# Nine regions instead of seven with a last product in quarters; the sums' room taken from s2, which is read back from DRAM; A in runs of 512 columns

## The chip, the cores and the metric

The kernel runs on one core of a Trainium2 chip. The metric is the device time of one execution in microseconds (us), the median of several runs.

## The reference

```python
m, k, n = 4096, 4096, 4096
x = np.matmul(a, b)                      # a, b: float32
return np.where(x > 0, x, alpha * x)     # alpha = 0.01
```

## The kernel before, in words

**Stages.** The inputs are rounded to fp16 on their way in. A is handled in four groups `g` of 1024 rows, B in four blocks `j` of 1024 columns. The 16 pairs (g, j) are done one after the other. The pair (0, 0) is done first in a stage of its own with plain products (line L295); the other 15 are called regions and come in this order: (0,1), (0,2), (0,3); (1,2), (1,0), (1,1), (1,3); (2,2), (2,0), (2,3), (2,1); (3,2), (3,0), (3,1), (3,3). In this text they are regions 0 to 14. The last region of each group is "turning": while it computes, the next group's A is loaded. Region 14 is the last one.

**A region.** It is one 2 x 2 step of a fast matrix product with seven products in place of eight. The four quarters of the group's A are a11, a12, a21, a22, each [512 rows x 2048 of k], in two tiles (k halves u); the four quarters of the block of B are b11, b12, b21, b22, each in two tiles of 1 MiB. Sums s1 to s4 of A's quarters are made on VectorE (DVE) once per group, sums of B's quarters in place in every region (`b_sum`, L574). The products (`PRODUCTS`), each 64 matmuls of 128 x 512 (L691), are numbered 0 to 6: a11 b11, a12 b21, s2 with a b11 sum, s3 with a b12 sum, s1 with another b11 sum, a22 with a b21 sum, s4 b22. Four PSUM banks `y` and four banks `z` take them in turn; ScalarE (ACT) copies a bank out (`keep`, L704), DVE adds (`add`, L746), applies the leaky step (L323), and SP stores.

**Quarters.** Where `in_quarters` holds, product 6 is split once more into seven parts of 16 matmuls of 128 x 256 (`quarters_product`, L722): 112 narrow matmuls in place of 64 wide ones. For that it needs sums of quarters of b22 (`tq`, four DVE operations in `sums_b`, L655 to L658) and of s4 (`sq`, made in the group's first region by `sums_s4` and kept in DRAM as `kept_s`; read back on SP in later regions). In the kernel before this holds in regions 3, 4, 7, 8, 11, 12 and 13. The room for `tq` and one `sq` is taken from b12's tiles (pool tag b12), so in these regions b12 of the next region can't be loaded before product 6 is done.

**Loads.** B and A come over POOL's queue, which converts fp32 to fp16: B in DMAs of 512 KiB (`fetch_unit`, two for a tile), A through staging tiles (pool a16, three of them, 4 KiB in a partition each, four DMAs each; L128) that DVE then transposes into place (L137). In group's first regions the block j = 2 of B is read back, already in fp16, from the DRAM copy `kept` on SP's queue. `fetch_b(i + 1, ...)` loads a quarter of the next region's B when the product that last reads it is done: b12 after product 3, b11 after 4, b21 after 5, b22 after 6; in quarter regions b12's two tiles come after product 6 too, mixed with b22's. In a turning region a11 of the next group is fetched and transposed after product 0's sums, a12 after product 1, a21 after 3, a22 after 5 (`fetch_a`). Each is four pieces; the fourth needs the staging tile of the first, so it is fetched when the first has been transposed. All engines work in the order of the program, and in turning regions DVE's order is: sums b12 and b11 (first k half, then second), transposes of a11, add and leaky of product 1, sum b21, transposes of a12, second sum b11, transposes of a21.

The second sum b11 (called b11'' here) must be there for product 4, the first one for product 2.

**Measuring.** The kernel also gathers the spread of the squares of every quarter of A and B (`Measure`: four ACT squares, about six DVE operations, held in a16 tiles) for a check at the end. `MEASURED` lists which quarter is measured where. Quarters of b that the region's in-place sums would have overwritten are measured a region ahead (entries `fifth`, `sixth`), or, twice, loaded a second time only to be measured (`MeasureApart`).

Of the kernel before, what the change touches and what calls it, by code (L numbers as in the profile page):

```python
# [8 lines left out]
P = 128  # L9
# [15 lines left out]
KC = 8  # L25
KW = KC * P
KU = 4
RUNS = [2, 1]
NT = 512
MT = 4  # L30
# [14 lines left out]
def kernel(  # L45
# [61 lines left out]
    def new_a(g, h, u):  # L107
        if (g, h, u) not in at:
            tag = f"a{h + 1}{u // 2 + 1}"
            at[g, h, u] = a_pool.tile([P, KC // 2, RM, 2], DT, name=tag, tag=tag)  # L110
        return at[g, h, u]
# [32 lines left out]

    def pieces_a(g, h, u, urgent=False):

        if u >= 2:
            return [whole_half(g, h, mt) for mt in range(MT) if u == 2]
        tiles = 2 * RUNS[u]
        kw = KW // RUNS[u]  # L150

        def piece(mt, tiles, r):
            def to(t0, t1):
                rows = slice((mt + t0) * P, (mt + t1) * P)
                return [new_a(g, h, u)[:, r * kw // P // 2:(r + 1) * kw // P // 2, rows, :]]
            row = ((g * 2 + h) * MT + mt) * P
            return load_a(row, u * KW + r * kw, kw, tiles, to)

        pieces = [piece(mt, tiles, r) for mt in range(0, MT, tiles) for r in range(RUNS[u])]
        if urgent:  # L160
            pieces[:1] = [piece(mt, 2, 0) for mt in range(0, MT, 2)]
        return pieces

    def whole_half(g, h, mt):
        def to(t0, t1):
            rows = slice((mt + t0) * P, (mt + t1) * P)
            return [new_a(g, h, u)[:, :, rows, :] for u in (2, 3)]
        return load_a(((g * 2 + h) * MT + mt) * P, 2 * KW, 2 * KW, 1, to)

    def b_rows(j, u, c, wide, nt=None):  # L170

        if u >= 2:
            per = 2 * KC
            k0 = 2 * KW
            c += u % 2 * KC
        else:
            per = KC // RUNS[u]
            k0 = u * KW + c // per * per * P
        n0 = j * 2 * NT + (nt or 0) * NT
        cols = slice(n0, n0 + (2 * NT if nt is None else NT))  # L180
        src = b[k0:k0 + per * P, cols].rearrange("(p c) n -> p c n", p=P)
        return src[:, c % per:c % per + wide, :]

    def load_b(j, u, c, wide, nt):
        nc.gpsimd.dma_start(new_b(j, u, nt)[:, c:c + wide, :], b_rows(j, u, c, wide, nt))
# [22 lines left out]
    class Measure:  # L208
# [12 lines left out]
        def square(self, n):  # L221
            to = self.place(n)
            nc.scalar.activation(to, self.parts[n], SQUARE)  # L223
            self.held.append(to)
# [5 lines left out]
        def end(self):  # L230
# [3 lines left out]
            nc.vector.tensor_add(total, total, more[1])  # L234
            nc.vector.tensor_add(total, total, self.held[3])  # L235
            fold(self.which, total, self.place(2), self.pairs)

    class MeasureApart(Measure):

        def load(self):
            self.loaded = [self.fetch(n) for n in range(3)]

        def fetch(self, n):
            to = self.place(n)
            half, nt, jb = self.parts
            nc.gpsimd.dma_start(
                to.bitcast(DT).rearrange("p (c n) -> p c n", n=NT),
                b_rows(jb, 2 * half + n // 2, n % 2 * 4, 4, nt))  # L250
            return to

        def square(self, n):
            to = self.loaded[n] if n < 3 else self.fetch(n)
            nc.scalar.activation(to, to.bitcast(DT), SQUARE)  # L255
            self.held.append(to)

    def fold(which, total, turned, pairs, weight=1.0):

# [237 lines left out]
            first_measure.end()  # L497


    kept = dram_pool.tile([KU, 2, P, KC * NT], DT, name="kept")  # L500
    regions = [(0, j) for j in range(1, J)]
    regions += [(g, j) for g in range(1, G) for j in ([2, 0, 3, 1] if g == 2 else [2, 0, 1, 3])]

# [8 lines left out]
    def fetch_unit(i, u, nt):  # L512
        g, j = regions[i]
        half = u // 2
        t = b_pool.tile([P, KC, NT], DT, name="b", tag=f"b{half + 1}{nt + 1}")
        have_b[i, u, nt] = t
        if g and j == CACHED:
            nc.sync.dma_start(t.rearrange("p c n -> p (c n)"), kept[u, nt])
        else:
            for c in range(0, KC, 4):  # L520
                nc.gpsimd.dma_start(t[:, c:c + 4, :], b_rows(j, u, c, 4, nt))  # L521
            if j == CACHED:
                nc.sync.dma_start(kept[u, nt], t.rearrange("p c n -> p (c n)"))

    have_b = {(0, u, nt): bt[1, u, nt] for u in range(2) for nt in range(2)}

    s = {}
    first_a = at[0, 0, 0]

    def flat(t):  # L530
# [13 lines left out]
        nc.vector.tensor_tensor(f(to), f(x0), f(x1), op)  # L544

    def new_s(g, name):
        t = x_pool.tile([P, 2, KC // 2, RM, 2], DT, name=name, tag="x")
        for k in range(2):
            s[g, name, k] = t[:, k]
        return t  # L550
# [22 lines left out]
        f = lambda t: t.rearrange("p c n -> p (c n)")  # L573
        nc.vector.tensor_tensor(f(to), f(x0), f(x1), op)  # L574

    def measure(i, which, x, y, jb=None, room=None):

        if jb is not None:
            return MeasureApart(which, (x, y, jb), False)
        if which:  # L580
            tiles = [have_b[i, 2 * x + k, y] for k in range(2)]
        else:
            tiles = [at[regions[i][0], x, 2 * y + k] for k in range(2)]
        parts = halves(tiles[0]) + halves(tiles[1])
        if tiles[0] is first_a:
            return MeasureFirst(which, parts, None)
        return Measure(which, parts, not which, room)

    def judge():
# [25 lines left out]
    A11, A12, A22 = (0, 0, 0), (0, 0, 1), (0, 1, 1)  # L615
    B11, B12, B21, B22 = ((1, half, nt) for half in range(2) for nt in range(2))
    MEASURED = {
        (0, 1): (None, [A11], B12, B11), (0, 2): (B21, [B22, A22], None, A12),
        (1, 2): (None, [A11], None, None), (1, 0): (B21, [B22, A12], None, None),
        (1, 1): (B21, [B22, A22], B12, B11),  # L620
        (2, 2): (None, [A11], None, None), (2, 0): (A12, [B11 + (0,)], None, None),
        (2, 3): (B21, [B22, A22], B12, B11),
        (3, 2): (None, [A11], None, None), (3, 0): (A12, [A22], None, None),
        (3, 1): (None, [B12 + (0,)], None, None),
    }

    PRODUCTS = [("a11", 0, 0), ("a12", 1, 0), ("s2", 0, 0), ("s3", 0, 1), ("s1", 0, 0), ("a22", 1, 0), ("s4", 1, 1)]


    HALF = NT // 2  # L630
    kept_s = dram_pool.tile([4, P, KC * HALF], DT, name="kept_s")
    side = 0

    def quarter_a(t):
# [1 line left out]

    def rooms(i):

        two = [b_pool.tile([P, 2, KC * HALF], DT, name="q", tag="b12") for _ in range(2)]
        three = [a16_pool.tile([P, KC * HALF], DT, name="sq4", tag="a16") for _ in range(3)]  # L640
        tq = {2: two[0][:, 0], 1: two[0][:, 1], 4: two[1][:, 0]}
        sq = {1: three[0], 2: three[1], 3: three[2], 4: two[1][:, 1]}
        return tq, sq
# [32 lines left out]
    for i, (g, j) in enumerate(regions):  # L676
# [98 lines left out]
        middle = middle and measure(i, *middle)  # L775
        late_ones = [measure(i, *x) for x in late_ones]
        first_of_group = i == 0 or regions[i - 1][0] != g
        next_turning = i + 2 < len(regions) and regions[i + 2][0] != g
        in_quarters = g > 0 and not turning and not next_turning and not final

        product(0, y, True)
        if middle:
            middle.begin()
        u1 = keep(y, side)
# [2 lines left out]
            b_sum(B(0, 0, k), B(0, 1, k), B(0, 0, k), ADD)  # L787
        if middle:
            middle.end()
        apart = late_ones and isinstance(late_ones[0], MeasureApart)  # L790
        if apart:
            late_ones[0].load()
        fetch_a(0, 0)

        product(1, z, True)
# [13 lines left out]
            b_sum(B(0, 0, k), B(1, 1, k), B(0, 0, k), SUB)  # L809
        if first_of_group:  # L810
            sum_a(g, "s4")
        if late_ones and not apart:
            late_ones[0].end()

        z = [new_bank(zbank + mt) for mt in range(MT)]
        product(3, z, True)
        v = keep(z, side)
        if not in_quarters:
            fetch_b(i + 1, [(0, 1)])
        fetch_a(1, 0)  # L820
        if apart:
            late_ones[0].end()
        for m in late_ones[1:]:
            m.begin()
            m.end()
        if in_quarters:
            tq, sq = rooms(i)
            if first_of_group:
                sums_s4(g, sq)
                sums_b(i, tq)  # L830

        product(4, y, False)
        a21 = None
        if turning:
            new_s(g + 1, "s1")
            t = new_s(g + 1, "s2").rearrange("p k c m e -> p (k c m e)").bitcast(BF16)
            a21 = measure(i + 1, 0, 1, 0, None, t.rearrange("p (n w) -> p n w", n=4))
            a21.begin()
        add(v, y)
        leave(v, 1, 1)  # L840
        if in_quarters and not first_of_group:
            for n in (4, 2, 1, 3):
                nc.sync.dma_start(sq[n], kept_s[n - 1])
            sums_b(i, tq)
        if a21:
            a21.end()
# [21 lines left out]

        if in_quarters:
            kept_c = quarters_product(i, y, new_bank(zbank + 2), new_bank(zbank + 3), tq, sq)  # L870
            for u, nt in ((3, 1), (0, 1), (2, 1), (1, 1)):
                fetch_unit(i + 1, u, nt)
            leave(kept_c, 0, 1)
        else:
            product(6, y, False)
            fetch_b(i + 1, [(1, 1)])
            if final:
                even = nc.values_load(good[0:1, 0:1], min_val=0, max_val=1)
            _, kept_c = new_c(side)

            def store(mt):
                nc.sync.dma_start(place(g, 0, mt, j, 1), kept_c[mt])

            for mt in range(MT):
                nc.scalar.copy(kept_c[mt], y[mt])  # L885
                leaky(kept_c[mt])
                if not (final and mt == MT - 1):
                    store(mt)
# [69 lines left out]
```

## Time and profile before

| what | value |
|---|---|
| median of 3 runs | 1574.33 us (1572.62 to 1574.84) |
| profiled execution | 1575.59 us, span 1573.5 us, granted clock 0.999 |
| TensorE busy (share of the span) | 1559.1 us (99%) |
| DVE, ACT, POOL busy | 1027.7, 372.6, 312.3 us |
| DMA: POOL's queue | 145.78 MB, 61.4% of 16 engines' span |
| DMA: SP's queue | 119.17 MB, 20.6% of 16 engines' span |

The span runs from the first to the last instruction; the 2.1 us between span and time lie around it. Megabytes of DMA are as written, so half of what was read where fp32 becomes fp16. In the timeline a row is a run of like instructions: start, length, engine, line, operation, and in square brackets the idle time before it and what ended it. A wide matmul is listed with 379 ns, but in a run they start every 216 ns; a narrow one is listed with 273 ns and they start every 109 ns.

### The profile page before, as it was taken

The numbers are of one execution on the slowest core, as the hardware profiler recorded it, in microseconds if no ns is written. First come the engines' busy times: TensorE is split into PE (matmuls) and PEld (weight loads), VectorE is DVE, ScalarE is ACT, GpSimd is POOL, SyncE is SP. The second block draws the span as 40 slices with busy tenths as digits, with TensorE's granted clock in tenths as the row PEclk, the third lists the DMA queues.
The fourth block names the chain that finished last, engine by engine and source line by source line (L and its number), as shares of the span: only waits on it lengthen the run. The fifth ranks groups of instructions, "written<-read, shape, count | busy, mean of one in ns | idle before, by whom it ended". The sixth has DMA issues, their size and how long they took to land. (4 is left out here: it accounts for less than half of the span.)

```text
span 1573.5 us, 19023 instructions
## 1 busy us (share of the span) xinstructions
PE 1559.1 (99%) x7611; PEld 743.1 (47%) x7611; DVE 1027.7 (65%) x1128; ACT 372.6 (24%) x390; POOL 312.3 (20%) x490
## 2 busy tenths in 40 slices
PE   9999999999999999999999999999999999999998
PEld 4444444444445445444444545544444454544543
DVE  4368758666975583877679475387877829455353
ACT  2201243412121332441221121263022123021110
POOL 5541110244002011024300201112520020201100
PEclk9999999999999999999999999999999999999999
DMA  9999695999609659499942977969992491995912
GB/s 244 188 206 191 137 286 153 191 204 194 226 28 225 123 110 253 92 205 168 253 149 85 224 133 168 194 110 227 168 255 102 119 234 44 211 204 105 249 35 83
DMA packets 224771, 266.64 MB, mean 169 GB/s; under 512 B 41633, under 2 KB 183201, under 8 KB 220578
## 3 DMA queue, kind: packets, MB, share of 16 engines
q0 software_dynamic: 178176, 145.78, 61.4%
q1 hardware_dynamic: 46210, 119.17, 20.6%
q8 instruction: 61, 1.00, 0.2%
q10 hardware_dynamic: 288, 0.39, 0.1%
q14 instruction: 36, 0.29, 0.0%
HBM read 327.16 MB, written 81.79 MB: 260 GB/s over the span
## 5 line engine op out<-in xcount | busy, mean ns | idle before, releaser
L691 PE MATMUL ps<-b,a 128*128 128x512 f16 x3840 | 836.3, 379 | 0.0
L691 PEld LDWEIGHTS <-a 128*128 128x128 f16 x3840 | 375.6, 98 | 451.9 <-issue 0.5
L691 PE MATMUL ps<-b,s 128*128 128x512 f16 x2432 | 531.2, 379 | 1.9 <-DVE b L574 1.9
L691 PEld LDWEIGHTS <-s 128*128 128x128 f16 x2432 | 237.6, 98 | 289.9 <-DVE b L574 3.9
L574 DVE TENSOR_TENSOR b<-b 128x4096 f16<-128x4096 f16 x112 | 252.7, 2288 | 163.1 <-DMA b<-in_b_dram 154.4
L521 POOL DMA_DIRECT2D b<-in_b_dram x184 | 136.5, 747 | 874.7 <-PE ps L691 695.4
L704 ACT COPY c<-ps 128x512 f32<-128x512 f32 x180 | 92.4, 598 | 493.9 <-PE ps L691 456.9
L746 DVE TENSOR_TENSOR c<-ps,c 128x512 f32<-128x512 f32 x180 | 111.6, 682 | 148.6 <-PE ps L691 100.3
L128 POOL DMA_DIRECT2D a<-in_a_dram x252 | 143.9, 579 | 173.6 <-DVE a L137 124.1
L137 DVE STREAM_TRANSPOSE a<-a 128x512 uint32<-128x512 uint32 (+2 forms) x96 | 115.2, 1240 | 87.7 <-DMA a<-in_a_dram 87.7
L323 DVE SCALAR_TENSOR_TENSOR c<-c 128x512 f32<-128x512 f32 x240 | 149.4, 685 | 17.6 <-ACT c L885 14.9
L223 ACT ACTIVATE sq<-b 128x2048 bf16<-128x2048 f16 x56 | 104.1, 1908 | 143.2 <-DVE sq L232 131.5
L295 PE MATMUL ps<-b,a 128*128 128x512 f16 x512 | 113.2, 379 | 3.1 <-DVE part L334 1.3
L223 ACT ACTIVATE sq<-a 128x2048 bf16<-128x2048 f16 x48 | 88.9, 1922 | 94.0 <-DVE sq L232 79.7
L295 PEld LDWEIGHTS <-a 128*128 128x128 f16 x512 | 49.7, 98 | 64.5 <-issue 6.0
L235 DVE TENSOR_TENSOR sq<-sq 128x2048 bf16<-128x2048 bf16 x27 | 33.1, 1225 | 31.8 <-ACT sq L255 16.3
L729 ACT COPY c<-ps 128x512 f32<-128x512 f32 x7 | 4.1, 586 | 196.7 <-PE ps L722 196.7
L885 ACT COPY c<-ps 128x512 f32<-128x512 f32 x32 | 16.7, 598 | 138.1 <-PE ps L691 138.1
L232 DVE TENSOR_TENSOR sq<-sq 128x2048 bf16<-128x2048 bf16 x27 | 33.0, 1221 | 9.5 <-ACT sq L223 9.5
L234 DVE TENSOR_TENSOR sq<-sq 128x2048 bf16<-128x2048 bf16 x27 | 33.1, 1226 | 5.0 <-ACT sq L223 2.3
L722 PEld LDWEIGHTS <-s 128*128 128x128 f16 x336 | 32.9, 98 | 5.3
L722 PEld LDWEIGHTS <-sq 128*128 128x128 f16 x336 | 32.9, 98 | 3.8
(88 smaller groups left out, 531.1 us busy)
## 6 DMA issues: line engine op xcount, KB each, us to landing
b<-in_b_dram POOLq DMA_DIRECT2D x192, 512.0 KB, 12.3
out_dram<-c SPq DMA_DIRECT2D x240, 256.0 KB, 5.5
a<-in_a_dram POOLq DMA_DIRECT2D x244, 128.0 KB, 5.4
b<-kept SPq DMA_DIRECT2D x24, 1024.0 KB, 7.8
kept<-b SPq DMA_DIRECT2D x8, 1024.0 KB, 7.8
b<-in_b_dram POOLq DMA_DIRECT2D x24, 256.0 KB, 9.7
sq<-kept_s SPq DMA_DIRECT2D x12, 512.0 KB, 12.4
kept_s<-sq SPq DMA_DIRECT2D x9, 512.0 KB, 2.8
```

Of the source, the lines that this page charges most:

```text
L128: nc.gpsimd.dma_start(a16[32 * q:32 * q + 32], src.rearrange("(g i) w -> i g w", i=32))
L137: nc.vector.transpose(part.rearrange("p c m e -> p c (m e)").bitcast(U32) .rearrange("p c (g i) -> p g c i", i=32), src[:, :, i * n:(i + 1 ...
L223: nc.scalar.activation(to, self.parts[n], SQUARE)
L234: nc.vector.tensor_add(total, total, more[1])
L295: nc.tensor.matmul(ps, a_cols(at[0, h, u], c, mt, (h, u) == (0, 0)), bt[0, u, nt][:, c, :], start=first, stop=last,)
L323: nc.vector.scalar_tensor_tensor(t, t, alpha, t, op0=MULT, op1=MAX if alpha <= 1 else MIN)
L521: nc.gpsimd.dma_start(t[:, c:c + 4, :], b_rows(j, u, c, 4, nt))
L574: nc.vector.tensor_tensor(f(to), f(x0), f(x1), op)
L691: nc.tensor.matmul(banks[mt], a_cols(t, c, mt, t is first_a), B(half, nt, k)[:, c, :], start=first and (k, c) == (0, 0), stop=(k, c) == (1 ...
L704: nc.scalar.copy(kept[mt], banks[mt])
L722: nc.tensor.matmul(to[m], xq[:, c // 2, rows, c % 2], yq[:, c, :], start=first and (c, m) == (0, 0), stop=c == KC - 1, skip_group_check=True,)
L746: nc.vector.tensor_add(acc[mt], banks[mt], acc[mt])
```

## The change

- `in_quarters` holds in nine regions: 3, 4, 5, 7, 8, 9, 11, 12, 13.
- The room for `tq` and one `sq` comes from pool x, where s2's tile is given up after product 2. s2 is stored once per group to `kept_s2` in DRAM (2 MiB) and read back on SP's queue after the quarters' product of each quarter region, for the next region's product 2.
- b12 of the next region is fetched after product 3 in every region. After the quarters' product only b22 is left to fetch.
- The `sq` of later regions are loaded after product 3, and `sums_b` moves ahead of product 4, except where two late quarters are measured (regions 4, 5, 9): there it stays behind product 4's add.
- A of groups 1 to 3 is loaded with k in pieces of 128 rows x 2048, runs of 512 columns, in both halves (before, the first half had runs of 128 and 256); B's rows and `kept` follow that order of k.
- b11 or b12 are measured in the region that uses them, ahead of product 0 (`EARLY`), in regions 5, 8, 9, 12, 13; the second loads are gone; region 1's b12 measurement is for region 2.

```diff
     def pieces_a(g, h, u, urgent=False):
-        if u >= 2:
-            return [whole_half(g, h, mt) for mt in range(MT) if u == 2]
+        if u >= 2 or g:
+            return [whole_half(g, h, mt, u // 2) for mt in range(MT) if u % 2 == 0]
...
-    class MeasureApart(Measure):
...
-    kept = dram_pool.tile([KU, 2, P, KC * NT], DT, name="kept")
+    kept = dram_pool.tile([2, KU * KW, NT], DT, name="kept")
...
-        (1, 1): (B21, [B22, A22], B12, B11),
-        (2, 2): (None, [A11], None, None), (2, 0): (A12, [B11 + (0,)], None, None),
-        (2, 3): (B21, [B22, A22], B12, B11),
+        (1, 1): (B21, [B22, A22], None, None),
+        (2, 2): (None, [A11], None, None), (2, 0): (A12, [], None, None),
+        (2, 3): (B21, [B22, A22], None, None),
         (3, 2): (None, [A11], None, None), (3, 0): (A12, [A22], None, None),
-        (3, 1): (None, [B12 + (0,)], None, None),
     }
+    EARLY = {(1, 1): B11, (2, 0): B11, (2, 3): B11, (3, 0): B12, (3, 1): B12}
...
+    kept_s2 = dram_pool.tile([P, 2 * KC * RM], DT, name="kept_s2")
...
     def rooms(i):
-        two = [b_pool.tile([P, 2, KC * HALF], DT, name="q", tag="b12") for _ in range(2)]
+        two = x_pool.tile([P, 2, 2, KC * HALF], DT, name="q", tag="x")
+        two = [two[:, 0], two[:, 1]]
...
-        next_turning = i + 2 < len(regions) and regions[i + 2][0] != g
-        in_quarters = g > 0 and not turning and not next_turning and not final
+        in_quarters = g > 0 and not turning and not final
+        early = measure(i, *EARLY[g, j]) if (g, j) in EARLY else None
+        if early:
+            early.begin()
+        if first_of_group and g:
+            nc.sync.dma_start(kept_s2, whole_s[g, "s2"].rearrange("p k c m e -> p (k c m e)"))
 
         product(0, y, True)
+        if early:
+            early.end()
...
         product(3, z, True)
         v = keep(z, side)
-        if not in_quarters:
-            fetch_b(i + 1, [(0, 1)])
+        fetch_b(i + 1, [(0, 1)])
         fetch_a(1, 0)
...
             if first_of_group:
                 sums_s4(g, sq)
+            else:
+                for n in (4, 2, 1, 3):
+                    nc.sync.dma_start(sq[n], kept_s[n - 1])
+            if len(late_ones) < 2:
                 sums_b(i, tq)
 
         product(4, y, False)
...
         leave(v, 1, 1)
-        if in_quarters and not first_of_group:
-            for n in (4, 2, 1, 3):
-                nc.sync.dma_start(sq[n], kept_s[n - 1])
+        if in_quarters and len(late_ones) == 2:
             sums_b(i, tq)
...
             kept_c = quarters_product(i, y, new_bank(zbank + 2), new_bank(zbank + 3), tq, sq)
-            for u, nt in ((3, 1), (0, 1), (2, 1), (1, 1)):
-                fetch_unit(i + 1, u, nt)
+            fetch_b(i + 1, [(1, 1)])
+            t = new_s(g, "s2")
+            nc.sync.dma_start(t.rearrange("p k c m e -> p (k c m e)"), kept_s2)
             leave(kept_c, 0, 1)
```

More of the change, by code (lines that the diff above doesn't have):

```diff
@@ L162, in pieces_a, with whole_half, rows_of @@
         return pieces
-    def whole_half(g, h, mt):
+    def whole_half(g, h, mt, half):
         def to(t0, t1):
             rows = slice((mt + t0) * P, (mt + t1) * P)
[L167 to L172, printed above, removed]
+            return [new_a(g, h, 2 * half + k)[:, :, rows, :] for k in range(2)]
+        return load_a(((g * 2 + h) * MT + mt) * P, half * 2 * KW, 2 * KW, 1, to)
+    def rows_of(mat, u, c, wide, whole):
+        if u >= 2 or whole:
             per = 2 * KC
-            k0 = 2 * KW
+            k0 = u // 2 * 2 * KW
             c += u % 2 * KC
@@ L178, in b_rows @@
             k0 = u * KW + c // per * per * P
+        return mat[k0:k0 + per * P, :].rearrange("(p c) n -> p c n", p=P)[:, c % per:c % per + wide, :]
+    def b_rows(j, u, c, wide, nt=None, whole=False):
         n0 = j * 2 * NT + (nt or 0) * NT
-        cols = slice(n0, n0 + (2 * NT if nt is None else NT))
-        src = b[k0:k0 + per * P, cols].rearrange("(p c) n -> p c n", p=P)
-        return src[:, c % per:c % per + wide, :]
+        return rows_of(b[:, n0:n0 + (2 * NT if nt is None else NT)], u, c, wide, whole)
     def load_b(j, u, c, wide, nt):
@@ L236, in end @@
             fold(self.which, total, self.place(2), self.pairs)
-    class MeasureApart(Measure):
[L242 to L256, printed above, removed]
     def fold(which, total, turned, pairs, weight=1.0):
@@ L517, in fetch_unit @@
         if g and j == CACHED:
-            nc.sync.dma_start(t.rearrange("p c n -> p (c n)"), kept[u, nt])
+            nc.sync.dma_start(t, rows_of(kept[nt], u, 0, KC, True))
         else:
             for c in range(0, KC, 4):
-                nc.gpsimd.dma_start(t[:, c:c + 4, :], b_rows(j, u, c, 4, nt))
+                nc.gpsimd.dma_start(t[:, c:c + 4, :], b_rows(j, u, c, 4, nt, g > 0))
             if j == CACHED:
-                nc.sync.dma_start(kept[u, nt], t.rearrange("p c n -> p (c n)"))
+                wide = KC // (RUNS + [1, 1])[u]
+                for c in range(0, KC, wide):
+                    nc.sync.dma_start(rows_of(kept[nt], u, c, wide, False), t[:, c:c + wide, :])
     have_b = {(0, u, nt): bt[1, u, nt] for u in range(2) for nt in range(2)}
     s = {}
+    whole_s = {}
     first_a = at[0, 0, 0]
@@ L546, in new_s @@
     def new_s(g, name):
-        t = x_pool.tile([P, 2, KC // 2, RM, 2], DT, name=name, tag="x")
+        t = whole_s[g, name] = x_pool.tile([P, 2, KC // 2, RM, 2], DT, name=name, tag="x")
         for k in range(2):
@@ L574, in b_sum, with measure @@
         nc.vector.tensor_tensor(f(to), f(x0), f(x1), op)
-    def measure(i, which, x, y, jb=None, room=None):
-        if jb is not None:
-            return MeasureApart(which, (x, y, jb), False)
+    def measure(i, which, x, y, room=None):
         if which:
@@ L617 @@
     MEASURED = {
-        (0, 1): (None, [A11], B12, B11), (0, 2): (B21, [B22, A22], None, A12),
+        (0, 1): (None, [A11], B12, B11), (0, 2): (B21, [B22, A22], B12, A12),
         (1, 2): (None, [A11], None, None), (1, 0): (B21, [B22, A12], None, None),
-        (1, 1): (B21, [B22, A22], B12, B11),
-        (2, 2): (None, [A11], None, None), (2, 0): (A12, [B11 + (0,)], None, None),
-        (2, 3): (B21, [B22, A22], B12, B11),
+        (1, 1): (B21, [B22, A22], None, None),
+        (2, 2): (None, [A11], None, None), (2, 0): (A12, [], None, None),
+        (2, 3): (B21, [B22, A22], None, None),
         (3, 2): (None, [A11], None, None), (3, 0): (A12, [A22], None, None),
-        (3, 1): (None, [B12 + (0,)], None, None),
     }
+    EARLY = {(1, 1): B11, (2, 0): B11, (2, 3): B11, (3, 0): B12, (3, 1): B12}
     PRODUCTS = [("a11", 0, 0), ("a12", 1, 0), ("s2", 0, 0), ("s3", 0, 1), ("s1", 0, 0), ("a22", 1, 0), ("s4", 1, 1)]
@@ L789 @@
             middle.end()
-        apart = late_ones and isinstance(late_ones[0], MeasureApart)
-        if apart:
-            late_ones[0].load()
         fetch_a(0, 0)
@@ L811 @@
             sum_a(g, "s4")
-        if late_ones and not apart:
+        if late_ones:
             late_ones[0].end()
@@ L817 @@
         v = keep(z, side)
-        if not in_quarters:
-            fetch_b(i + 1, [(0, 1)])
+        fetch_b(i + 1, [(0, 1)])
         fetch_a(1, 0)
-        if apart:
-            late_ones[0].end()
         for m in late_ones[1:]:
@@ L836 @@
             t = new_s(g + 1, "s2").rearrange("p k c m e -> p (k c m e)").bitcast(BF16)
-            a21 = measure(i + 1, 0, 1, 0, None, t.rearrange("p (n w) -> p n w", n=4))
+            a21 = measure(i + 1, 0, 1, 0, t.rearrange("p (n w) -> p n w", n=4))
             a21.begin()
```

## The prediction

> **What bounds the kernel now.** I read the page's first section, then the waits, then timelines at two places, then the DMA rates. TensorE (PE) is busy 99% of the span, and between regions 0 and 14 only one kind of wait reaches it (waits: engine, line, releaser, us in total, times, longest):
>
> ```profile
> PE 1559.1 (99%) x7611; PEld 743.1 (47%) x7611; DVE 1027.7 (65%) x1128; ACT 372.6 (24%) x390; POOL 312.3 (20%) x490
> ```
> ```profile
> PE ps L691 <- DVE b L574: 1.9, 4, 0.6
> DVE b L574 <- DMA b<-in_b_dram: 158.1, 21, 19.1
> ```
>
> So the time is a count of matmuls plus small stalls, and a change gains by taking matmuls away or loses by making PE wait. The timeline of PE around the end of region 4, a quarter region, shows both what quarters save and where the stalls come from:
>
> ```profile
> 592.41 3.66 PE L722 MATMUL ps<-b,s 128*128 128x256 f16 x32
> ...
> 604.64 27.79 PE L691 MATMUL ps<-b,a 128*128 128x512 f16 x128
> 632.98 1.25 PE L691 MATMUL ps<-b,s 128*128 128x512 f16 x5 [0.55 <-DVE b L574]
> ```
>
> The narrow product 6 takes from 592.41 to 604.64. In region 5 product 2 starts late, since the sum of b11 waits for b12 and b22, which were loaded only after the quarters. The turning regions show a chain that has little slack. This is DVE in region 6, which starts at 702.26:
>
> ```profile
> 716.18 4.69 DVE L574 TENSOR_TENSOR b<-b 128x4096 f16<-128x4096 f16 x2 [2.69 <-DMA a<-in_a_dram]
> 720.78 2.46 DVE L137 STREAM_TRANSPOSE a<-a 128x1024 uint32<-128x1024 uint32 x2
> 724.58 2.03 DVE L137 STREAM_TRANSPOSE a<-a 128x1024 uint32<-128x1024 uint32 x1 [1.33 <-DMA a<-in_a_dram]
> 729.02 2.03 DVE L137 STREAM_TRANSPOSE a<-a 128x1024 uint32<-128x1024 uint32 x1 [2.41 <-DMA a<-in_a_dram]
> 730.98 2.44 DVE L746 TENSOR_TENSOR c<-ps,c 128x512 f32<-128x512 f32 x4
> 733.34 2.49 DVE L323 SCALAR_TENSOR_TENSOR c<-c 128x512 f32<-128x512 f32 x4
> 735.74 4.49 DVE L574 TENSOR_TENSOR b<-b 128x4096 f16<-128x4096 f16 x2
> 740.14 6.08 DVE L137 STREAM_TRANSPOSE a<-a 128x512 uint32<-128x512 uint32 x6
> 748.83 2.10 DVE L137 STREAM_TRANSPOSE a<-a 128x512 uint32<-128x512 uint32 x2 [2.61 <-DMA a<-in_a_dram]
> 750.86 2.25 DVE L574 TENSOR_TENSOR b<-b 128x4096 f16<-128x4096 f16 x1
> ```
>
> From 716.18, when the second half of b22 is there, the rows follow one another: b sums, four transposes of a11 (the fourth piece is fetched when the first is transposed: POOL starts that at 722.32, and it lands 6.7 us later), add, leaky, a sum, a12 the same way (fourth piece fetched at 742.54, landed at 748.83), and then b11'', whose first half is there at 753.1. Product 4, which reads it, starts at 757.51: 4.4 us of slack. In region 10 the same chain runs from 1099.97 to 1138.1 before a product at 1141.9: 3.8 us. Counted from the region's start the second half of b22 is used at +13.9 and +13.3.
>
> The last view is of rates (windows: PE, PEld, DVE, ACT, POOL busy, clock, DMA share, GB/s):
>
> ```profile
> 587.00:590.00 3.00, 3.00 (x15) 1.37 (x14) 0.83 (x1) 0.00 (x0) 0.69 (x1) 1.00 1.10 359
> 605.00:608.00 3.00, 3.00 (x16) 1.36 (x14) 3.00 (x7) 3.00 (x3) 0.82 (x2) 1.00 1.26 213
> 617.00:620.00 3.00, 3.00 (x16) 1.35 (x15) 0.00 (x0) 1.99 (x4) 0.00 (x0) 1.00 1.24 206
> 782.00:785.00 3.00, 3.00 (x16) 1.35 (x15) 1.00 (x5) 0.00 (x0) 0.00 (x0) 1.00 0.98 412
> ```
>
> POOL's queue alone moves 206 GB/s, SP's alone (reading `kept`) 412. From 587 to 590 both have work, and 0.95 of the 1.07 MB were SP's `sq` loads: POOL's transfers nearly stop while SP's run.
>
> **Part by part. Two more quarter products (regions 5, 9).** A plain product 6 takes 13.81 us (region 5: 688.45 to 702.26), one in quarters 12.23 (above). 2 x 1.58 = 3.2 us gained, all on PE's path.
>
> **b12 fetched after product 3.** Eight units of 1 MiB no longer crowd behind product 4; at 206 GB/s a unit takes 5.1 us, and units come free every 6.9 us (half a product). After the quarters only two are left instead of four. DVE's sum in region 5 starts at 628.24, 23.6 us into the region; with this order I expect the first half of b22 at about +14 and the first b11 sum at +18.6, with product 2 at +27.7. The four stalls go: 1.9 us, plus 0.16 each (379 ns of listed length less the 216 ns step), 2.6 us in all. What is late next there is s2, below.
>
> **s2 by DRAM.** Three stores of 2 MiB (regions 3, 7, 11) find no POOL traffic beside them, and SP's earlier stores stand ahead of them in its queue: nothing. Nine loads are issued on SP when the last narrow matmul is done; behind them stand four stores of product 6, which DVE's leaky step releases 3 to 5 us later anyway. A load needs 2.10 MB / 412 GB/s = 5.1 us, and some 2.8 us to start (750.85 to 753.7 for a `kept` load): there at about +8, product 2 needs it at +27.7. The slowest `sq` load lands 14.6 us after its issue; that holds too. On PE nothing.
>
> But it delays b22. In region 5 as it will be, the first half of b22 comes free 1.3 us before the end (POOL issued such a load at 603.35 for 604.64), and data flow 1.3 to 2.0 us after an issue. Then two units (2.10 MB / 206 = 10.2 us), s2 (5.1 us) and the stores of product 6 (1.05 MB at 388 GB/s, the rate from 684 to 686: 2.7 us) share the DMA engines: 18.0 us from +0.4, and 1.8 us from the last data to DVE (data end at 631.6 in region 5, DVE goes on at 633.42). The second half is there at +20.2, 6.3 us later than in region 6 now and 6.9 later than in region 10. In quarter regions that costs nothing: b sums end at +25, product 2's second half starts at +34.6. In the turning regions 6 and 10 it pushes the chain above.
>
> **A in runs of 512.** The a11 transposes become the a12 form: 6.08 us for six, 2.05 for a piece, where the first piece now takes about 1.2: 0.9 us more ahead of the fourth piece's fetch. That piece now moves 1 KiB runs instead of 512 B; the fourth piece of a12, which has them already, landed 6.3 us after the start of its fetch instead of 6.7: 0.4 us less, and I allow 0.7. So region 6 is late by 6.3 + 0.9 - 0.7 - 4.4 = 2.1 us at product 4, region 10 by 6.9 + 0.2 - 3.8 = 3.3. Together 5.4 us lost. Region 2 follows a plain region: its 4.2 us of slack (368.8 for 373.0) covers the 0.2.
> The price hangs on +20.2. If POOL's queue shared better or b22 landed by +17, it would be nothing; with 2 us of units left over from b21, which is free only at 83 us of 95, it is +22 and 9 us.
>
> **The rest costs nothing, with its cover.** `sums_b` earlier: four DVE operations of 1.22 us, done some 57 us into the region, and the next thing on DVE, product 4's add, waits for PE until 69. `sq` loads earlier: they wait for staging tiles until the last late measure, about 70 us into the region, and SP's stores of product 4 wait behind them; used at 87. Early measures: ACT has 5.7 us of squares ahead of `keep`, which must end at +27.7; DVE 6.3 us, done by +12, ahead of sums that wait for b22 until +14. If b22 came early these 6 us would lie open, and product 2's slack of 9 us would take them. The dropped second loads were off the path.
>
> One rule of the Trainium skill speaks against this change. First the rows: from 605 to 608 DVE was busy all 3.00 us and DMA moved 213 GB/s; from 617 to 620 DVE was idle and it moved 206. The skill's page "SBUF — State Buffer" (the trap that DVE blocks DMA) says that POOL's descriptors can't be written while DVE runs its two-port modes, so transfers of that queue stall behind DVE work. By that rule the fetches behind the longer transposes and early measures would slip by the length of those operations; by the rows they don't, and I add nothing.
>
> **Sum.** Against the profiled 1575.59 (1.26 above the median): -3.2 - 2.6 + 5.4 = -0.4. Against the median: 1574.33 - 0.4 = 1573.9.
>
> **Rivals.**
> 1. *The slack holds.* If b22's second half lands before about +18.9, the turning regions lose under 2.7 us in all, and at +17 nothing: 1574.33 - 5.8 = 1568.5. For it: staging and POOL's ring may let a11 land sooner than now; PE hides all else. Against: SP's traffic went first from 587 to 590.
> 2. *The chain in regions 6 and 10 decides the other way.* Each us after +20 counts twice. At +23, with b21's last unit still in the queue when the quarters end, the loss is 11 us: 1574.33 - 5.8 + 11 = 1579.5. It decides from +22 on. For it: 42 of the 45 us before the quarters' end are filled with transfers by the same rates (six units 31 us, `sq` 5.1, stores 5.5).
> 3. *The skill's rule* (above) holds for the fetch of the fourth pieces: behind three more transposes of 2.05 us each in both regions, 12 us: 1574.33 - 0.4 + 12 = 1586. The rows give it little.
> 4. *The stalls at product 2 stay*, because s2 takes the place of b12: gain 3.2, loss 5.4: 1576.5.
>
> **Numbers.** About 0.2% (3.1 us) is what a measurement of this kernel can tell from no change. My forecast, a loss in two regions that gives back most of the gain: 0.40 (1571 to 1577). Rival 1: 0.34, counted as faster. Rival 2: 0.18, rival 3: 0.03, both slower. Rival 4: 0.05, of which 0.03 within the bound and 0.02 slower. So 0.34 faster, 0.43 same, 0.23 slower. The range of 1568 to 1579.5 takes in rivals 1 and most of 2.
>
> **What would show it.** Right: 1008 narrow matmuls (784 before); no wait of L691 for L574 at product 2 in regions 5, 9, 13, 14; b22's second sum near +20 after a quarter region; PE idle at product 4 of regions 6 and 10, ended by DVE L574, of 2 to 3 us each. Wrong: no such idle time (rival 1), or an idle PE at product 2 released by an SP load of s2, or at the narrow matmuls.

## The result, and the profile after

The changed kernel takes 1583.85 us (median of 5, 1582.06 to 1586.05) against 1574.33 (five runs as well, 1572.62 to 1575.9): 1.0062 of the time before, interval 1.0047 to 1.0076. It is slower by 9.5 us, where no change was forecast. The profiled execution took 1586.05 us, 10.5 more than that of before.

First the page of the changed kernel, busy times and the new DMA group, then its waits (L680 is the L691 of before, L561 the b sums, L574 before; further down L139 is the transposes, L137 before, L735 the add and L307 the leaky step):

```profile
PE 1559.8 (98%) x7707; PEld 754.0 (48%) x7707; DVE 1055.6 (67%) x1172; ACT 372.6 (24%) x390; POOL 299.5 (19%) x482
```
```profile
s<-kept_s SPq DMA_DIRECT2D x9, 2048.0 KB, 10.4
```
```profile
PE ps L680 <- DVE b L561: 12.6, 2, 6.6
DVE b L561 <- DMA b<-in_b_dram: 83.9, 22, 10.6
```

The wait of PE has moved: four short ones have become two long ones. The timeline of PE shows where, in region 6 at product 4:

```profile
740.02 13.98 PE L680 MATMUL ps<-b,a 128*128 128x512 f16 x64
760.07 16.93 PE L680 MATMUL ps<-b,s 128*128 128x512 f16 x64 [6.07 <-DVE b L561]
776.83 13.54 PE L680 MATMUL ps<-b,a 128*128 128x512 f16 x62
```

In this view product 3 starts at 740.02, product 4 at 760.07 and product 5 at 776.83. Product 3 takes 13.82 us, so product 4 was due at 753.84. It starts 6.2 us late. It also lasts 16.76 us to the start of product 5, which is 2.9 too long. The windows view (PE, PEld, DVE, ACT, POOL busy, clock, DMA share, GB/s) shows the clock, and the traffic ahead of the gap, which is read further down:

```profile
746.00:749.00 3.00, 3.00 (x16) 1.37 (x14) 3.00 (x4) 0.00 (x0) 2.78 (x6) 1.00 0.46 49
749.00:752.00 3.00, 3.00 (x16) 1.37 (x14) 0.88 (x1) 0.00 (x0) 2.04 (x5) 1.00 1.01 322
...
760.00:763.00 3.00, 2.93 (x7) 1.03 (x8) 3.00 (x3) 0.00 (x0) 0.27 (x1) 0.50 1.15 217
```

From 760 to 763 the granted clock is 0.50, and it stays there until 766: after the idle time 14 matmuls go by at 427 ns instead of 216. Region 10 is the same: product 4 was due at 1145.03 and is 6.7 us late, and 8 slow matmuls cost 1.7 us.

```profile
1151.75 15.66 PE L680 MATMUL ps<-b,s 128*128 128x512 f16 x64 [6.56 <-DVE b L561]
```

Last, DVE in region 6, which now starts at 698.58:

```profile
712.88 4.69 DVE L561 TENSOR_TENSOR b<-b 128x4096 f16<-128x4096 f16 x2 [9.74 <-DMA b<-in_b_dram]
719.51 4.69 DVE L561 TENSOR_TENSOR b<-b 128x4096 f16<-128x4096 f16 x2 [1.95 <-DMA a<-in_a_dram]
724.12 6.05 DVE L139 STREAM_TRANSPOSE a<-a 128x512 uint32<-128x512 uint32 x6
732.64 2.10 DVE L139 STREAM_TRANSPOSE a<-a 128x512 uint32<-128x512 uint32 x2 [2.47 <-DMA a<-in_a_dram]
...
743.84 6.04 DVE L139 STREAM_TRANSPOSE a<-a 128x512 uint32<-128x512 uint32 x6
755.77 2.07 DVE L139 STREAM_TRANSPOSE a<-a 128x512 uint32<-128x512 uint32 x2 [5.89 <-DMA a<-in_a_dram]
757.76 4.45 DVE L561 TENSOR_TENSOR b<-b 128x4096 f16<-128x4096 f16 x2
```

It is the chain of the prediction, row for row: b22's second half at +20.9 (719.51), transposes of a11, add, leaky and sum, a12, b11''. (The bracket at 719.51 names A's load, but the landing in the trace just ahead of it, at 719.39, is that of b22's last 512 KiB, so the row is read as b22's.) One wait has grown: DVE waits 5.89 us for the fourth piece of a12, where it waited 2.61 before. POOL starts that fetch at 746.22, and it lands 9.55 us later, not 6.3. SP issues the load of `kept` for the next region's b12 at 747.12. Between 750 and 752 the packets of the trace are 0.74 MB of SP's and 0.02 of POOL's.

**Sum over the span.** Gained: 3.2 us by the quarters, 2.6 by the four stalls, which are gone; region 0 began 1.2 us sooner in this execution (123.18 against 124.35). That is scatter: over the nine traces of this text it begins between 121.8 and 124.4, and in before_sum_first below, which has the old code up to there, at 122.35. Lost: 6.2 + 6.7 idle, 2.9 + 1.7 at half clock. -7.0 + 17.5 = 10.5, and the spans differ by 10.7.

### The profile page after: what moved, and what is told of

Its sections match the earlier page's. It is cut to its first block, busy times and chain, and to the rows that moved or that the text cites. A ratio compares the mean times of both kernels' runs of the same rounds, so it can differ in the third digit from the quotient of the medians.

```text
span 1584.2 us, 19332 instructions
## 1 busy us (share of the span) xinstructions
PE 1559.8 (98%) x7707; PEld 754.0 (48%) x7707; DVE 1055.6 (67%) x1172; ACT 372.6 (24%) x390; POOL 299.5 (19%) x482
## 5 line engine op out<-in xcount | busy, mean ns | idle before, releaser
L680 PE MATMUL ps<-b,a 128*128 128x512 f16 x3840 | 836.1, 379 | 0.0
L680 PEld LDWEIGHTS <-a 128*128 128x128 f16 x3840 | 375.6, 98 | 451.2
L680 PE MATMUL ps<-b,s 128*128 128x512 f16 x2304 | 507.8, 381 | 12.6 <-DVE b L561 12.6
L680 PEld LDWEIGHTS <-s 128*128 128x128 f16 x2304 | 226.5, 98 | 288.4 <-DVE b L561 13.6
L561 DVE TENSOR_TENSOR b<-b 128x4096 f16<-128x4096 f16 x112 | 252.9, 2289 | 91.4 <-DMA b<-in_b_dram 80.4
L735 DVE TENSOR_TENSOR c<-ps,c 128x512 f32<-128x512 f32 x180 | 111.7, 683 | 200.6 <-PE ps L680 133.1
L139 DVE STREAM_TRANSPOSE a<-a 128x512 uint32<-128x512 uint32 (+2 forms) x120 | 125.9, 1100 | 77.8 <-DMA a<-in_a_dram 77.6
L130 POOL DMA_DIRECT2D a<-in_a_dram x252 | 137.3, 551 | 201.5 <-DVE a L139 126.8
L307 DVE SCALAR_TENSOR_TENSOR c<-c 128x512 f32<-128x512 f32 x240 | 149.4, 685 | 12.7 <-ACT c L877 10.0
L227 ACT ACTIVATE sq<-b 128x2048 bf16<-128x2048 f16 x64 | 119.0, 1909 | 87.8 <-DVE sq L236 74.0
L711 PEld LDWEIGHTS <-sq 128*128 128x128 f16 x432 | 42.2, 98 | 4.9
L877 ACT COPY c<-ps 128x512 f32<-128x512 f32 x24 | 12.6, 598 | 119.6 <-PE ps L680 119.6
```

The lines of the kernel that those rows point to most:

```text
L130: nc.gpsimd.dma_start(a16[32 * q:32 * q + 32], src.rearrange("(g i) w -> i g w", i=32))
L139: nc.vector.transpose(part.rearrange("p c m e -> p c (m e)").bitcast(U32) .rearrange("p c (g i) -> p g c i", i=32), src[:, :, i * n:(i + 1 ...
L307: nc.vector.scalar_tensor_tensor(t, t, alpha, t, op0=MULT, op1=MAX if alpha <= 1 else MIN)
L680: nc.tensor.matmul(banks[mt], a_cols(t, c, mt, t is first_a), B(half, nt, k)[:, c, :], start=first and (k, c) == (0, 0), stop=(k, c) == (1 ...
L711: nc.tensor.matmul(to[m], xq[:, c // 2, rows, c % 2], yq[:, c, :], start=first and (c, m) == (0, 0), stop=c == KC - 1, skip_group_check=True,)
L735: nc.vector.tensor_add(acc[mt], banks[mt], acc[mt])
```

## The experiments

**Theories.** *Chain:* s2's load and the late release of b22 push the in-order DVE chain of regions 6 and 10 past product 4; once late, its last fetch meets the `kept` load and is held up further, and PE's idle time costs clock. *Form of A:* the a11 transposes and the runs of 512 make the chain late. *Spread:* the added SP traffic slows the regions at large. All ratios are to the kernel before on the same chip.

**seven**: regions 5 and 9 plain again, the rest as changed.

```diff
-        in_quarters = g > 0 and not turning and not final
+        next_turning = i + 2 < len(regions) and regions[i + 2][0] != g
+        in_quarters = g > 0 and not turning and not next_turning and not final
```

> Regions 5 and 9 keep a plain product 6, so no s2 load ahead of the turning regions 6 and 10; all else as changed. Chain theory (s2's load and the late release of b22 push the turning regions' DVE chain past product 4): b22's second half is used near +14 in regions 6 and 10 instead of +21, no idle PE at product 4, no half clock; the four stalls of before at product 2 stay away: 1574.3 - 2.6 = 1571.7. Rival 'form of A' (the two-part transposes of a11 and runs of 512 make the chain late): PE idle of 6 us at product 4 of regions 6 and 10 stays, about 1583 + 3 = 1586. Rival 'spread' (the added SP traffic slows all regions): about 1579, half way back.

1572.6 us, 0.9986 (0.9977 to 0.9995). PE waits for no b sum any more. DVE in region 6, which starts at 701.41:

```profile
714.03 4.69 DVE L561 TENSOR_TENSOR b<-b 128x4096 f16<-128x4096 f16 x2 [3.22 <-DMA b<-in_b_dram]
...
749.11 4.46 DVE L561 TENSOR_TENSOR b<-b 128x4096 f16<-128x4096 f16 x2
```

b22's second half is used at +12.6, and b11'' has its first half at 751.4 for a product 4 at 756.66. The whole loss hangs on the two added quarter regions; the new form of A, the early b12 and seven s2 loads by themselves gain 1.9 us (interval 0.8 to 3.6) where 2.6 were expected. The form of A and the spread both fall here.

**sum_first**: the chain's order alone.

```diff
-        fetch_a(0, 1)
 
         product(2, y, False)
...
             b_sum(B(0, 0, k), B(1, 1, k), B(0, 0, k), SUB)
+        fetch_a(0, 1)
```

> In turning regions DVE makes the second b11 sum before it transposes a12; no other edit to the changed kernel. Chain theory: DVE is free for it near +45, it is done by +50, product 4 starts at +55.3 without a wait, clock stays full: 1574.3 - 3.2 - 2.6 = 1568.5. Rival 'too much work for DVE and DMA in a turning region': the wait only moves, to the a21 pieces or to s1 and s2 of the next group (product 2 of regions 7 and 11), and the time stays above 1578.

1567.85 us, 0.9957 (0.9944 to 0.9971). DVE in region 6, which starts at 699.11:

```profile
740.22 8.89 DVE L561 TENSOR_TENSOR b<-b 128x4096 f16<-128x4096 f16 x4
749.03 6.07 DVE L139 STREAM_TRANSPOSE a<-a 128x512 uint32<-128x512 uint32 x6
```

The two operations of sum b21 and those of b11'' now run as one row, done at 749.1, 5 us ahead of product 4 at 754.37. The page's waits have no L680 for PE. b22 is as late as in the changed kernel (719.59, +20.5) and the traffic is the same; only who stands behind the late fetch has changed. The full 5.8 us that the prediction's gains add up to are there (6.6 by the medians).

**s2_made**: s2 is made again from s1 and a11 on DVE; no load, no store.

```diff
-        if first_of_group and g:
-            nc.sync.dma_start(kept_s2, whole_s[g, "s2"].rearrange("p k c m e -> p (k c m e)"))
...
-            t = new_s(g, "s2")
-            nc.sync.dma_start(t.rearrange("p k c m e -> p (k c m e)"), kept_s2)
             leave(kept_c, 0, 1)
+            new_s(g, "s2")
+            sum_a(g, "s2")
```

> s2 is made again on DVE (s1 - a11, two operations of 2.3 us) after the quarters' product instead of loaded from DRAM; no store of s2; nine quarter regions stay. If s2's 2 MiB ahead of b22 is the cause: b22's second half is used near +16 in regions 6 and 10 instead of +21, the chain ends 5 us earlier and its last fetch clear of the kept load, no idle PE at product 4: 1568.5. If the late release of b22 by the quarters is the cause: used at +19 or later, PE still idle 3 us or more, 1576 or above.

1568.12 us, 0.9960 (0.9946 to 0.9973). DVE in region 6, which starts at 697.62:

```profile
702.10 4.48 DVE L531 TENSOR_TENSOR s<-s,a 128x4096 f16<-128x4096 f16 x2
706.50 4.68 DVE L561 TENSOR_TENSOR b<-b 128x4096 f16<-128x4096 f16 x2
712.95 4.69 DVE L561 TENSOR_TENSOR b<-b 128x4096 f16<-128x4096 f16 x2 [1.77 <-DMA b<-in_b_dram]
...
749.58 4.45 DVE L561 TENSOR_TENSOR b<-b 128x4096 f16<-128x4096 f16 x2
```

s2 takes 4.48 us of a DVE that was waiting anyway, and b22's second half is used at +15.3. So of the 7.0 us by which the changed kernel is late (+20.9 for +13.9), 5.6 are s2's load (5.2 in region 10). The other 1.4 are what the late release of b22 costs less what the rest of the change gains: against seven, which has all but the two quarter products and their loads, the late release is 2.7 us (+15.3 for +12.6; 2.0 in region 10). This is the suspected cost taken away alone, and the loss goes with it.

**kept_late**: the `kept` load of b12 after product 4 in turning regions.

```diff
-        fetch_b(i + 1, [(0, 1)])
+        if not turning:
+            fetch_b(i + 1, [(0, 1)])
...
-        fetch_b(i + 1, [(0, 0)])
+        fetch_b(i + 1, [(0, 1), (0, 0)] if turning else [(0, 0)])
```

> In turning regions the kept copy of b12 is loaded after product 4 instead of after product 3; no other edit to the changed kernel. If that load holds back the fetch of a12's fourth piece: the piece lands 6.3 us after the start of its fetch instead of 9.6 and 10.5, PE's idle time falls from 6.1 and 6.6 us to about 2.8, and with it perhaps the 3 and 2 us at half clock: 1583.9 - 7 to - 12 = 1572 to 1577. If the load has nothing to do with it: the piece lands as late as before and the time stays at 1583.

1578.16 us (1575.93 to 1580.0), 1.0025 (1.0014 to 1.0035), 5.7 below the changed kernel and a little above what was expected. DVE and PE in region 6, then windows behind the two gaps:

```profile
743.54 6.08 DVE L139 STREAM_TRANSPOSE a<-a 128x512 uint32<-128x512 uint32 x6
751.95 2.09 DVE L139 STREAM_TRANSPOSE a<-a 128x512 uint32<-128x512 uint32 x2 [2.32 <-DMA a<-in_a_dram]
```
```profile
756.27 15.45 PE L680 MATMUL ps<-b,s 128*128 128x512 f16 x64 [3.12 <-DVE b L561]
```
```profile
756.00:759.00 3.00, 2.73 (x7) 1.01 (x8) 3.00 (x3) 0.00 (x0) 0.48 (x1) 0.50 1.24 201
...
1143.20:1146.20 3.00, 2.72 (x13) 1.29 (x14) 3.00 (x3) 0.00 (x0) 0.49 (x1) 1.00 1.21 190
```

POOL starts the fourth fetch at 745.95 and it is there at 751.95: 6.0 us instead of 9.55 (in region 10 6.7 instead of 10.5). The idle times halve, to 3.12 and 3.57 us. So the `kept` load is worth some 3 us in each region, and this part of the price is shown. The clock dropped after the gap of 3.12 us and not after the one of 3.57. This profiled execution is the fastest of the eight, with a granted clock of 0.998; the others have 0.995 to 0.997, so most of them lost more to the clock, and they spread over 4 us.

**a_old**: the changed kernel with A's first half in the old runs (and B's rows and `kept` in the old order).

```diff
-        if u >= 2 or g:
+        if u >= 2:
...
-                nc.gpsimd.dma_start(t[:, c:c + 4, :], b_rows(j, u, c, 4, nt, g > 0))
+                nc.gpsimd.dma_start(t[:, c:c + 4, :], b_rows(j, u, c, 4, nt))
```

> The changed kernel with A's first half (and B's rows and kept with it) in the old runs of 128 and 256 columns; everything else as changed. Chain theory: the a11 transposes ahead of the fourth fetch are 0.9 us shorter, the transfers of a11 4 to 5 us longer; the fetch of a12's fourth piece still starts behind the kept load, PE idles 5 to 8 us at product 4 of regions 6 and 10 with half clock behind it: 1582 to 1587. Rival 'form of A': with the old form the idle time is gone, about 1569.

1583.08 us, 1.0063 (1.0049 to 1.0077): the same as changed. The chain in region 6 (DVE, then PE):

```profile
742.69 6.07 DVE L139 STREAM_TRANSPOSE a<-a 128x512 uint32<-128x512 uint32 x6
754.46 2.07 DVE L139 STREAM_TRANSPOSE a<-a 128x512 uint32<-128x512 uint32 x2 [5.70 <-DMA a<-in_a_dram]
```
```profile
758.75 15.44 PE L682 MATMUL ps<-b,s 128*128 128x512 f16 x64 [6.09 <-DVE b L563]
```

The idle time is 6.09 us for 6.07, and 5.66 for 6.56 in region 10. The runs of 512 neither made nor cured the loss.

**before_sum_first**: the kernel before with the order of sum_first (the same edit).

> The kernel before, with the second b11 sum ahead of a12's transposes in turning regions and no other edit. Chain theory: the chain had 4 us of slack there, so nothing changes: 1574.3, and the gain of sum_first came from the changed kernel's own wait. Rival (the old order cost something in every turning region, so that 'sum_first' is a gain of its own): 1571 or less.

1574.44 us, 0.9999 (0.9990 to 1.0008). Nothing, as expected: there the chain had its 4 us of slack. The four stalls at product 2 are still there:

```profile
PE ps L691 <- DVE b L574: 2.7, 4, 1.3
```

So the gain of sum_first is that of the change itself, set free. This trace also shows the collision without s2 and without two more quarter products: b11'' goes first, so POOL starts the fourth fetch of region 6 at 746.42, SP issues the `kept` load at 748.78, and the piece is there 10.6 us after its start. PE does not wait, since b11'' no longer stands behind it.

**both**: s2_made and sum_first together.

> The changed kernel with both mends: s2 made again on DVE, and the second b11 sum ahead of a12's transposes. If each mend alone already takes away the whole wait, the two together bring nothing more: 1567.9 as each alone. If some loss is left that each hides in part (DMA, DVE): 1566 or less.

1568.53 us, 0.9964 (0.9951 to 0.9978). Each mend alone already takes away the whole wait; two bring no more. The late fetch is back in region 6 (started at 744.87, `kept` load at 746.60, there at 755.70), and PE does not wait for it.

Over all nine traces, regions 6 and 10, the fourth fetch took 9.0 to 10.8 us in the eight cases where the `kept` load was issued 0.7 to 2.4 us behind its start, and 6.0 to 7.1 us in the ten others (5.6 us or more behind, 3.1 to 3.8 ahead, or no load beside it).

## Why the prediction was wrong, point by point

- **Quarters, 3.2 us, and the four stalls, 2.6 us:** right. PE's waits at product 2 are gone, and sum_first and s2_made, which have the change without its new wait, are faster than before by 0.43% and 0.40%; 5.8 us would be 0.37%.
- **s2 itself hidden:** right, with room to spare. The six loads of the nine whose landing the trace has take 9.8 to 10.9 us from their issue, 2 to 3 us longer than the +8 that was forecast, and no product 2 waits.
- **b22's second half at +20.2:** right, +20.9 in region 6 and +20.4 (1110.15 for a region that starts at 1089.8) in region 10. The sum of the transfer times of s2, b22 and the stores held.
- **The place of the loss, product 4 of regions 6 and 10:** right, and only there.
- **Its size, 5.4 us: wrong**, and this put the forecast on the wrong side. Two terms were mis-sized. First, the fourth piece of a12 got no term of its own: it was taken to land 6.3 us after the start of its fetch, as it did before. But before, that piece had landed (748.83) when the `kept` load was issued (750.85); moved 7 us later against product 3, it ran into it and took 9.55 and 10.5 us. With that, region 6 gives 7.0 (b22) + 0.4 (the a11 transposes) + 3.2 (the fourth piece) - 4.4 (slack) = 6.2 and region 10 7.1 + 0.1 + 3.4 - 3.8 = 6.8, against 6.2 and 6.7 measured. The terms that the forecast had, b22 and the a11 transposes, came within 1 us. I had shown that SP's transfers nearly stop POOL's, and did not ask which transfers the chain's later steps are moved into. Second, a lost microsecond of PE was priced at one microsecond; the half clock behind each gap made it 4.6 us more. No run changes the clock alone; but between the start of region 0 and the last matmul the nine traces have half clock only at such a gap. Idle 12.9 and clock 4.6 are 17.5 in place of 5.4.
- **Rival 2** (slower, by the chain in regions 6 and 10) is what happened, but not by its cause: it had b22 at +23 behind a last unit of b21. b22 came on time.
- **Rival 3, the rule** of the Trainium skill's page "SBUF — State Buffer" on POOL's descriptors behind DVE work: DVE's work did not hold these transfers up. In s2_made DVE was busy 10.08 of 11 us while b22 was loaded, and the transfers went on at 247 GB/s (windows view), of which POOL's queue had 1.65 MB and SP's stores 1.05 MB; from 702.2 to 703.6, without SP's, the DMA moved 214 GB/s with DVE busy throughout.

```profile
701.00:712.00 11.00, 11.00 (x53) 4.99 (x51) 10.08 (x6) 1.01 (x3) 1.63 (x3) 1.00 1.19 247
```

Which of DVE's operations here run in the two-port modes that the rule speaks of, no run shows, so the rule itself is not tested.

- **Early measures, earlier `sums_b`, earlier `sq` loads:** nothing, right: no other wait of PE appeared.

What stays open: how long a gap brings the clock down for certain.

## What to carry to other kernels

When a step is late against a schedule, follow it to the transfers that it now meets: slack read from a trace holds only while the later steps stay clear of other queues, and past that point a delay grows. On an engine that works in order, look first at who stands behind a waiting step without needing it; moving one sum ahead of the transposes turned 0.6% slower into 0.4% faster. And a stall of the engine that bounds the kernel, here PE, can cost more than its length.

## What the runs showed of the hardware that was not expected

- **The clock after a gap.** PE idle for 6.07 us was followed by 14 matmuls at 427 ns (granted clock 0.50), 6.56 us by 8 of them, 6.09 us (a_old) by 7, 3.12 us by 7, 3.57 us by none. The Trainium skill's page "TensorE: Matmul & The Clock Gate" (Part 1) says that an idle window of about 3.4 us halves the clock, that a window of busy work brings it back, and that the windows run freely. The halving and the chance in it agree; a gap of 3.12 us is a little shorter than the page's window and was enough once.
- **Where the gap lies seems to count, not its length alone.** In the changed kernel the clock is at 0.50 from 759.22 to 766.05 and from 1148.34 to 1155.17, 6.83 us each time. PE was still idle for 0.85 us of the first stretch and for 3.41 of the second, hence 14 slow matmuls and 8. The other stretches last 6.83 or 3.41 us (kept_late: 755.84 to 759.25), and the two of the changed kernel start 389.12 us apart, 114 times 3.41. Counted in such steps, 2.7 us of kept_late's gap of 3.12 fall into one step, and its gap of 3.57 is split into 1.6 and 1.9. That fits what the clock did; no run moves a gap to show it.
- **SP's transfers went first.** With 8 KiB rows on SP's queue and 1 KiB writes on POOL's, 0.74 MB against 0.02 moved in 2 us (750 to 752), and in region 10 0.88 against 0.22 in 4 us (1141 to 1145).
